# The first microseconds of an encoder layer in a pinned order, with GpSimd on three weight splits and a shorter Newton step

## The chip, the cores and the metric

One core of a Trainium2 chip runs the whole program. Its engines are TensorE (PE; its weight loads are shown as PEld), VectorE (DVE), ScalarE (ACT), GpSimd (POOL) and SyncE (SP), which here only issues DMAs. The metric is the device time of one execution in microseconds (us), the median of the runs.

## The reference, cut to what matters

One layer of an encoder trunk on x of 512 rows by 1024 columns, in float32:

```python
h = rms_norm(x, norm_mix_pre)              # x * rsqrt(mean(x*x) + 1e-6) * g
z = h @ w_in                               # 1024 x 10240
za, zb, q, k, v, su, sv, gl = split(z)
a = za * sigmoid(zb)                       # then a depthwise convolution, layer norm, silu
y_a = a @ w_proj_conv
y_b = rms_norm(diff_attention(q, k, v)) @ w_proj_attn
y_c = spatial_gating(gelu(su), layer_norm(gelu(sv))) @ w_proj_sgu
mix = (g_a * y_a + g_b * y_b + g_c * y_c) @ w_out      # g: sigmoid gates from gl
x = x + rms_norm(mix, norm_mix_post)
f = square(relu(rms_norm(x, norm_ffn_pre) @ w_ffn_up)) @ w_ffn_down
x = x + rms_norm(f, norm_ffn_post)
```

## The kernel before

**Matrix products.** Every operand of a large product is split into a high part, rounded by ScalarE to the matmul's input type, and a low part, the difference, made by VectorE. A product is then three matmuls: high by high, high by low, low by high (`mm3`). A "unit" (`unit_gen`) is a 128-column block of weights against all 512 rows of h, eight steps of three matmuls. A weight block of 128 x 1024 numbers goes through `load_to` (L139 to L152): a DMA on SP's queue into `raw` (L149), the high part `w_hi` on ScalarE (L150), the low part `w_lo` on VectorE (L151). There are three buffers each for raw, high and low. `take` hands out the next blocks and loads ahead. The list `specs` holds the order of all weight blocks; its first three are the pair zb, za of convolution channel block 0 and zb of block 1.

**Order.** A scheduler puts each engine's instructions in order by their place in the program, their readiness and priorities. TensorE's matmuls and transposes are pinned in program order. The helper `keep_in_program_order` ties an instruction behind the one that was written before it on the same engine.

**The head.** ScalarE's queue loads the norm's scales `gpre`, one row copied to all 128 partitions (L271). VectorE clears a tile `zero`, and TensorE multiplies it 26 times as a warm-up (`keep_warm`, L277). SP issues the four 128-row tiles of x (`xx`, L287), with the first weight block behind tile 1 (`W0AT = 1`), the other weight blocks after tile 3.

`norm_x(t)` then norms a tile of x: square with the row sum on ScalarE (L297), `rstd_of`, and the scaling by the row's factor and `gpre` on VectorE (`hs`, L303). `to_T` turns the tile with eight transposes on TensorE (L62), in two halves of a PSUM bank each. ScalarE writes each half's high part `hh` (L223), VectorE its low part `hl` (L224). Tiles 0 and 1 come first, each followed by a few warm-up matmuls of `zero`. Then come the first units on columns 0 to 255, which are tiles 0 and 1: unit 0, norm of tile 2, unit 1, norm of tile 3, unit 2. The second halves of the three units follow, on columns 256 to 511. Unit 0's first half has its own order: eight matmuls of high by high, then eight with the weight's low part, then eight with `hl`. For tiles 2 and 3 a hand-written edge puts the square behind the last `hh` of the tile two before.

**The root.** `rstd_of` (L196) gives 1/sqrt(scale * ss + eps): v on VectorE (L199), ScalarE's root (L201), VectorE's reciprocal (L203) as the first guess, then a Newton step in three VectorE instructions (L206, L210, L211): s = v * r * r, s = 1.5 - 0.5 * s, r = r * s. Where n > 1 the first of them takes two. `eps_with` (L190) adds the first half of a mean to eps, for rows whose squares come in two halves: the norm behind w_out (L815 to L818, its tiles then scaled in L827, turned by `to_T`) and the last norm (`finish`, L1247 to L1258), where VectorE scales and adds (`us`, L1257) and the output is stored.

**Other work on GpSimd.** The constants, the identity for the transposes, seven small loads into `prow` and `cw` (L331 to L339), the padding of `apad` (L359, L360), four small loads for lambda (L187) and an iota (L434).

Of the kernel before, what the change touches and what calls it, by code (L numbers as in the profile page):

```python
# [26 lines left out]
EPS = 1e-6  # L27
# [14 lines left out]
W0AT = 1  # L42
# [6 lines left out]
def encoder_layer(ctx: ExitStack, tc: tile.TileContext, a: dict, out: bass.AP):  # L49
    nc = tc.nc  # L50
    vec, act, pool = nc.vector, nc.scalar, nc.gpsimd
# [15 lines left out]
    def f32(ap):  # L67
        return ap.bitcast(F32)
# [70 lines left out]
    def load_to(n):  # L139
        while len(loaded) < min(n, len(specs)):  # L140
# [10 lines left out]
            vec.tensor_tensor(lo, raw, f32(hi[:, :]), op=ALU.subtract)  # L151
# [38 lines left out]
    def eps_with(p, ss, scale):  # L190

        e = p.tile([P, 1], F32, tag="rs_e", bufs=4, name="rs_e")
        vec.tensor_scalar(e, ss, scale, EPS, op0=ALU.mult, op1=ALU.add)
        return e

    def rstd_of(p, ss, scale, eps=EPS, eps_tile=None, n=1, steps=1):  # L196

        v = p.tile([P, n], F32, tag=f"rs_v{n}", bufs=4 if n == 1 else 1, name="rs_v")
        vec.tensor_scalar(v, ss, scale, eps, op0=ALU.mult, op1=ALU.add)  # L199
        s = p.tile([P, n], F32, tag=f"rs_s{n}", bufs=4 if n == 1 else 1, name="rs_s")  # L200
        act.activation(s, ss, AF.Sqrt, bias=eps_t if eps_tile is None else eps_tile, scale=scale)  # L201
        r = p.tile([P, n], F32, tag=f"rs_r{n}", bufs=4 if n == 1 else 1, name="rs_r")
        vec.reciprocal(r, s)  # L203
        for _ in range(steps):
            if n == 1:
                vec.scalar_tensor_tensor(s, v, r, r, op0=ALU.mult, op1=ALU.mult)  # L206
            else:
                vec.tensor_tensor(s, v, r, op=ALU.mult)
                vec.tensor_tensor(s, s, r, op=ALU.mult)
            vec.tensor_scalar(s, s, -0.5, 1.5, op0=ALU.mult, op1=ALU.add)  # L210
            vec.tensor_tensor(r, r, s, op=ALU.mult)  # L211
        return r

    def to_T(src, hi, lo, tt):
        for half in range(2):
            b = bank("b")
            for j in range(4):
                kt = half * 4 + j
                pe.transpose(b[:, j * P:(j + 1) * P], src[:, kt * P:(kt + 1) * P], ident)
            b3 = b.rearrange("p (k t) -> p k t", t=P)  # L220
            c = slice(half * 4, half * 4 + 4)
            tk = slice(tt * P, (tt + 1) * P)
            ev = act.activation(hi[:, c, tk], b3, AF.Copy)  # L223
            vec.tensor_tensor(lo[:, c, tk], b3, f32(hi[:, c, tk]), op=ALU.subtract)  # L224
        return ev.ins

    def mm3(o, s, m, first, last):

# [39 lines left out]
    hl = KOf(held("hl", "hl", F32R))  # L268
    with mk("p0") as p0:
        gpre = p0.tile([P, D], F32, tag="gpre", name="gpre")  # L270
        act.dma_start(gpre, a["norm_mix_pre"].partition_broadcast(P))  # L271
        warm = p0.tile([P, 1], F32, tag="warm", name="warm")
        act.activation(warm, eps_t, AF.Sqrt)
        zero = p0.tile([P, S], F32R, tag="zero", name="zero")
        vec.memset(f32(zero[:, :]), 0.0)

        def keep_warm(n):  # L277

            b = bank("b")
            for _ in range(n):  # L280
                pe.matmul(b, zero[:, 0:P], zero, start=True, stop=True)

        keep_warm(26)
        xt = []
        for t in range(TT):
            xx = p0.tile([P, D], F32, tag="xx", bufs=4, name="xx")
            nc.sync.dma_start(xx, x[t * P:(t + 1) * P, :])  # L287
            xt.append(xx)
            if t == W0AT:
                load_to(1)  # L290

        evac = {}

        def norm_x(t):
            sq = p0.tile([P, D], F32, tag="sq", bufs=2, name="sq")
            ss = p0.tile([P, 1], F32, tag="ss", bufs=4, name="ss")
            i = act.activation(sq, xt[t], AF.Square, accum_out=ss)  # L297
            if t > 1:
                tc.add_manual_dep(i.ins, evac[t - 2].name, mybir.DependencyInfo(
                    mybir.DependencyClass.NoSync, mybir.DependencyReason.DATA), reason="order")  # L300
            r = rstd_of(p0, ss, 1.0 / D)
            hs = p0.tile([P, D], F32, tag="hs", bufs=2, name="hs")
            vec.scalar_tensor_tensor(hs, xt[t], r, gpre, op0=ALU.mult, op1=ALU.mult)  # L303
            evac[t] = to_T(hs, hh, hl, t)


        hT = (hh, hl)
        norm_x(0)
        keep_warm(3)
        norm_x(1)  # L310
        keep_warm(2)
        first = take(3, 0)
        fb = [bank("a") for _ in first]
        for n, w in enumerate(first):
            if n == 0:

                for i, (sw, m) in enumerate(((0, 0), (1, 0), (0, 1))):
                    for kt in range(KT):
                        pe.matmul(fb[0][:, 0:256], w[sw][:, kt], hT[m][:, kt, 0:256], start=i + kt == 0,
                                  stop=(i, kt) == (2, KT - 1))  # L320
            else:
                run(unit_gen(fb[n][:, 0:256], w, hT, slice(0, 256)))
            if n < 2:
                norm_x(2 + n)
        for n, w in enumerate(first):
            run(unit_gen(fb[n][:, 256:512], w, hT, slice(256, 512)))


        rowsrc = [("conv_b", 8), ("conv_ln_g", 8), ("conv_ln_b", 8), ("b_gate", 24), ("subln_g", 1), ("sgu_b", 8)]
        prow = p0.tile([P, P], F32, tag="prow", name="prow")  # L330
        pool.memset(prow, 0.0)  # L331
        off, col = 0, {}
        for n, k in rowsrc:
            pool.dma_start(prow[off:off + k, :], a[n].rearrange("(r c) -> r c", c=P) if len(a[n].shape) == 1 else a[n])
            col[n] = off
            off += k
        cw = p0.tile([32, D], F32, tag="cw", name="cw")
        pool.memset(cw, 0.0)
        pool.dma_start(cw[0:CK, :], a["conv_w"])  # L339
        pcol = cq.tile([P, P], F32, tag="pcol", name="pcol")  # L340
        b = bank("b")
        pe.transpose(b[:, 0:P], prow, ident)
        for c in range(KT):
            pe.transpose(b[:, P + c * 32:P + (c + 1) * 32], cw[:, c * P:(c + 1) * P], ident[0:32, 0:32])
        vec.tensor_copy(pcol, b[:, 0:P])
        convw = cq.tile([P, KT, 32], F32, tag="convw", name="convw")
        vec.tensor_copy(convw, b[:, P:P + KT * 32].rearrange("p (k j) -> p k j", j=32))

        def pc(n, i=0):
            return pcol[:, col[n] + i:col[n] + i + 1]  # L350
# [203 lines left out]
    for h in range(H):  # L554
        n = 0
# [230 lines left out]
    with mk("p4") as p4:  # L786
# [21 lines left out]
        for t in range(TT):  # L808
            for i in range(4):
                out_mm(b1, t, i, ws[i])  # L810
                if (t, i) in TURN:
                    to_T(h2s[TURN[t, i]], h2h, h2l, TURN[t, i])
            ss = p4.tile([P, 2], F32, tag="ss", bufs=4, name="ss")
            u, jk = wk[:, t], p4.tile([P, D], F32, tag="jk", bufs=3, name="jk")
            act.activation(jk[:, 0:512], b0[t], AF.Square, accum_out=ss[:, 0:1])  # L815
            e = eps_with(p4, ss[:, 0:1], 1.0 / D)
            act.activation(jk[:, 512:], b1[t], AF.Square, accum_out=ss[:, 1:2])
            r = rstd_of(p4, ss[:, 1:2], 1.0 / D, e, e)  # L818
            for i, bs in enumerate((b0, b1)):
# [7 lines left out]
            vec.scalar_tensor_tensor(jk, u, r2, gpre2, op0=ALU.mult, op1=ALU.mult)  # L827
            h2s.append(jk)
# [412 lines left out]
    def finish(nh, t, xs=None):  # L1241
# [9 lines left out]
        if nh == 0:  # L1251
            es.append(eps_with(cp, ss[:, t, 0:1], 1.0 / D))
            return
        r = rstd_of(cp, ss[:, t, 1:2], 1.0 / D, es[t], es[t])
        for e, i in ((nc.sync, 0), (act, 1)):
            hf = slice(i * 512, (i + 1) * 512)
            vec.scalar_tensor_tensor(us[t // 2][:, t % 2, hf], us[t // 2][:, t % 2, hf], r, xs[t // 2][:, t % 2, hf], op0=ALU.mult, op1=ALU.add)  # L1257
# [80 lines left out]
```

## Time and profile before

| | us |
|---|---|
| median of 3 runs | 1060.11 |
| lowest, highest | 1059.85, 1064.0 |
| profiled execution | 1059.99 |
| its span | 1058.2 |
| TensorE busy | 1042.6 |
| VectorE, ScalarE, GpSimd busy | 827.0, 580.5, 24.3 |

The span runs from the first to the last instruction of the profiled execution. The execution's own time is 1.8 us longer than it. Matmuls are pipelined and their ends are modelled, so the busy time of TensorE says that it was occupied, not that it ran at its peak.

A row of the timeline has the start, the duration, the engine, the line, the operation, the tile written and the tiles read, the shape and the count. At its end stands in brackets the engine's idle time before it, with what ended it. A row of the DMA view has the tile, the queue, the count, the size and the time from issue to landing.

### The profile page before, as it was taken

To read this page: it belongs to the slowest core of one execution; us is meant where nothing else is said; L and a number is where in the kernel's file an instruction comes from. 1 tells how busy PE (TensorE), PEld (TensorE's weight loads), DVE (VectorE), ACT (ScalarE), POOL (GpSimd) and SP (SyncE) were. 2 spreads that over 40 slices of the span, in tenths; PEclk is the share of its full clock that TensorE was granted. 3 is DMA by queue.
4 is the path that set the end of the run, shared out by engine and by line. 5 is a ranking of instruction groups with operands and counts; after the bars stand their busy time and mean duration, and the time that the engine had idled before them with its cause. 6 is when DMAs were issued, how large, how long until landed. Compare 5 with 4: busy or idle time off the path is not lost.

```text
span 1058.2 us, 14724 instructions
## 1 busy us (share of the span) xinstructions
PE 1042.6 (99%) x5688; PEld 900.0 (85%) x5688; DVE 827.0 (78%) x1296; ACT 580.5 (55%) x902; POOL 24.3 (2%) x41
## 2 busy tenths in 40 slices
PE   8999999999999999999999999999999999999997
PEld 7989898888878888888888888888999999888885
DVE  6696887968997697999899546457988889867746
ACT  5456677766673752344322493344677787555531
POOL 3000000000000000000000000000000001100000
PEclk9999999999999999999999999999999999999999
DMA  7342323223232333322333214463343319724532
GB/s 227 84 139 61 100 81 100 80 81 87 73 120 87 92 112 90 99 81 80 100 100 99 80 45 135 132 226 138 112 150 101 122 43 265 150 80 139 178 121 80
DMA packets 138391, 118.15 MB, mean 112 GB/s; under 512 B 4166, under 2 KB 116850, under 8 KB 138321
## 3 DMA queue, kind: packets, MB, share of 16 engines
q1 hardware_dynamic: 133120, 103.82, 32.1%
q0 software_dynamic: 4480, 11.82, 4.8%
q10 hardware_dynamic: 720, 1.57, 0.4%
q8 instruction: 44, 0.72, 0.3%
q14 instruction: 27, 0.21, 0.1%
HBM read 108.81 MB, written 4.19 MB: 107 GB/s over the span
## 4 chain that ended last, share of the span: by engine, by line
PE 91%; DVE 5%; ACT 2%; issue 1%; DMA 1%; DVEq 0%; ACTq 0%
PE ps_a L58 69%; PE ps_b L58 19%; PE ps_b L62 3%; DVE w_lo L951 1%; DMA xx<-in_x_dram 1%; DVE us L1257 0%; DVE w_lo L151 0%; ACT y L751 0%; DVE hs L303 0%; DVE jk L827 0%; PE ps_a L62 0%; DVE hl L224 0%; ACT jk L825 0%; DVE jk L1247 0%; DVE rs_s L206 0%
## 5 line engine op out<-in xcount | busy, mean ns | idle before, releaser
L150 ACT ACTIVATE w_hi<-w_raw 128x1024 fp32r<-128x1024 f32 x116 | 122.9, 1059 | 214.0 <-PE ps_a L58 177.4
L58 PE MATMUL ps_a<-hh,w_hi 128*128 128x512 f32 (+1 forms) x536 | 205.4, 385 | 0.0
L58 PE MATMUL ps_a<-hh,w_lo 128*128 128x512 f32 (+1 forms) x536 | 202.9, 381 | 0.0
L58 PE MATMUL ps_a<-hl,w_hi 128*128 128x512 f32 (+1 forms) x536 | 202.5, 380 | 0.0
L372 DVE SCALAR_TENSOR_TENSOR acc<-apad,convw,acc 128x512 f32<-128x512 f32 x232 | 173.5, 748 | 5.0
L151 DVE TENSOR_TENSOR w_lo<-w_raw,w_hi 128x1024 fp32r<-128x1024 f32 x116 | 141.5, 1220 | 41.5 <-ACT w_hi L150 41.2
L58 PEld LDWEIGHTS ps_a<-hh,w_lo 128*128 128x128 f32 x536 | 100.3, 188 | 19.6
L58 PEld LDWEIGHTS ps_a<-hl,w_hi 128*128 128x128 f32 x536 | 100.4, 188 | 18.3
L58 PEld LDWEIGHTS ps_a<-hh,w_hi 128*128 128x128 f32 x536 | 100.4, 188 | 18.2
L58 PE MATMUL ps_a<-ring,w_hi 128*128 128x256 f32 x336 | 57.9, 276 | 0.0
L58 PEld LDWEIGHTS ps_a<-ring,w_hi 128*128 128x128 f32 x336 | 50.6, 188 | 0.0
L58 PE MATMUL ps_a<-h2h,w_lo 128*128 128x256 f32 x176 | 48.8, 277 | 1.4 <-DVE w_lo L951 1.4
L58 PE MATMUL ps_a<-w_hi,hh 128*128 128x256 f32 (+1 forms) x160 | 49.7, 311 | 0.0
L58 PE MATMUL ps_a<-h2h,w_hi 128*128 128x256 f32 x176 | 49.0, 278 | 0.0
L58 PE MATMUL ps_a<-h2l,w_hi 128*128 128x256 f32 x176 | 48.8, 277 | 0.0
L58 PE MATMUL ps_a<-w_hi,hl 128*128 128x256 f32 (+1 forms) x160 | 48.7, 304 | 0.0
L58 PE MATMUL ps_a<-w_lo,hh 128*128 128x256 f32 (+1 forms) x160 | 48.6, 304 | 0.0
L507 ACT ACTIVATE e<-ps_b,m 128x512 f32<-128x512 f32 x64 | 43.4, 681 | 7.3 <-DVE m L503 7.0
L58 PE MATMUL ps_a<-ring,w_lo 128*128 128x256 f32 x168 | 46.5, 277 | 0.2 <-DVE w_lo L951 0.2
L58 PE MATMUL ps_a<-w_hi,ring 128*128 128x512 f32 x144 | 45.5, 389 | 0.0
L503 DVE CUSTOM_DVE_ANT_0 ps_b<-ps_b,al 128x512 f32<-128x512 f32 x64 | 43.5, 698 | 0.5 <-PE ps_b L58 0.2
L951 DVE TENSOR_TENSOR w_lo<-w_raw,w_hi 128x1024 fp32r<-128x1024 f32 x28 | 33.7, 1220 | 8.3 <-ACT w_hi L947 8.3
(304 smaller groups left out, 2431.6 us busy)
## 6 DMA issues: line engine op xcount, KB each, us to landing
w_raw<-in_w_in_dram SPq DMA_DIRECT2D x80, 512.0 KB, 3.7
w_raw<-in_w_ffn_up_dram SPq DMA_DIRECT2D x32, 512.0 KB, 4.6
w_raw<-in_w_ffn_down_dram SPq DMA_DIRECT2D x28, 512.0 KB, 4.1
w_raw<-in_w_proj_attn_dram SPq DMA_DIRECT2D x8, 512.0 KB, 4.0
w_raw<-in_w_proj_sgu_dram SPq DMA_DIRECT2D x8, 512.0 KB, 4.1
w_raw<-in_w_proj_conv_dram SPq DMA_DIRECT2D x8, 512.0 KB, 4.1
w_raw<-in_w_out_dram SPq DMA_DIRECT2D x8, 512.0 KB, 3.6
t<-in_w_ffn_down_dram SPq DMA_DIRECT2D x8, 512.0 KB, 5.7
```

The source lines that it names most:

```text
L58: return tc.keep_in_program_order(nc.tensor.matmul(*args, **kw))
L62: return tc.keep_in_program_order(nc.tensor.transpose(*args, **kw))
L150: act.activation(hi, raw, AF.Copy)
L151: vec.tensor_tensor(lo, raw, f32(hi[:, :]), op=ALU.subtract)
L372: vec.scalar_tensor_tensor(o, apad[:, c, j:j + S], convw[:, c, j:j + 1], acc, op0=ALU.mult, op1=ALU.add)
L503: vec.tensor_tensor_reduce(b, b, nal[:, 384 - q * P:896 - q * P], 1.0, 3.0e38, ALU.add, ALU.min, m)
L507: act.activation(e, b, AF.Exp, bias=m, scale=-1.0, accum_out=l)
L951: order(vec.tensor_tensor(lo, raw, f32(hi[:, :]), op=ALU.subtract))
```

## The change

- **Loads.** `gpre` is issued by SP behind tiles 0 and 1 of x, no longer by ScalarE. Raw weight block 0 follows it, then tile 2, block 1, tile 3, block 2.
- **Order.** The square, the root, the scaling, the first three weight splits, `hh` and `hl` are pinned in the order written. ScalarE has: square 0, root 0, square 1, root 1, hi 0, hh 0, hh 1, square 2, root 2, hi 1, square 3, root 3, hi 2, hh 2, hh 3. VectorE has: root and hs of tile 0, root and hs of tile 1, hl 0, hl 1, root and hs of tile 2, root and hs of tile 3, hl 2, hl 3. TensorE's order stays.
- **Low parts.** The low parts of the first three weight blocks are made by GpSimd (`pool.tensor_tensor`).
- **Newton.** v is made with the factor -0.5, so a step is s = v * r * r and r = (s + 1.5) * r, one instruction fewer. `eps_with` gives eps and -0.5 * eps, one VectorE instruction more.

```diff
+    def first_raw():
+        raw = wp.tile([P, 1024], F32, tag="raw", bufs=3, name="w_raw")
+        nc.sync.dma_start(raw.rearrange("p (k c) -> p k c", c=P), specs[len(heads)])
+        heads.append(raw)
+    def first_parts(n, eng):
+        hi = wp.tile([P, 1024], F32R, tag="hi", bufs=3, name="w_hi")
+        lo = wp.tile([P, 1024], F32R, tag="lo", bufs=3, name="w_lo")
+        eng(act.activation(hi, heads[n], AF.Copy))
+        pool.tensor_tensor(lo, heads[n], f32(hi[:, :]), op=ALU.subtract)
+        loaded.append([t.rearrange("p (k c) -> p k c", c=P) for t in (hi, lo)])
+        return loaded[-1]
...
-        return e
+        eh = p.tile([P, 1], F32, tag="rs_h", bufs=4, name="rs_h")
+        vec.tensor_scalar(eh, e, -0.5, None, op0=ALU.mult)
+        return e, eh
...
-        vec.tensor_scalar(v, ss, scale, eps, op0=ALU.mult, op1=ALU.add)
+        eng(vec.tensor_scalar(v, ss, -0.5 * scale, both[1], op0=ALU.mult, op1=ALU.add))
...
-            vec.tensor_scalar(s, s, -0.5, 1.5, op0=ALU.mult, op1=ALU.add)
-            vec.tensor_tensor(r, r, s, op=ALU.mult)
+            eng(vec.scalar_tensor_tensor(r, s, 1.5, r, op0=ALU.add, op1=ALU.mult))
...
-        act.dma_start(gpre, a["norm_mix_pre"].partition_broadcast(P))
...
             if t == W0AT:
-                load_to(1)
+                nc.sync.dma_start(gpre, a["norm_mix_pre"].partition_broadcast(P))
+                first_raw()
+            elif t > W0AT:
+                first_raw()
...
-        norm_x(0)
+        first = []
+        h0 = scaled(0, root(0))
+        r = root(1)
+        first.append(first_parts(0, pinned))
+        h1 = scaled(1, r)
+        to_T(h0, hh, hl, 0, pinned)
         keep_warm(3)
-        norm_x(1)
+        to_T(h1, hh, hl, 1, pinned)
         keep_warm(2)
-        first = take(3, 0)
+        h2_ = scaled(2, root(2))
+        first.append(first_parts(1, pinned))
+        h3_ = scaled(3, root(3))
+        first.append(first_parts(2, pinned))
...
             if n < 2:
-                norm_x(2 + n)
+                to_T((h2_, h3_)[n], hh, hl, 2 + n, pinned)
+        taken[0] = 3
```

Here `root(t)` is the square with `rstd_of`, `scaled(t, r)` the scaling, both pinned, and `to_T` pins its `hh` and `hl`.

More of the change, by code (lines that the diff above doesn't have):

```diff
@@ L152, in load_to @@
             loaded.append((hi.rearrange("p (k c) -> p k c", c=m), lo.rearrange("p (k c) -> p k c", c=m)))
+    heads = []
+    def first_raw():
[9 more added lines that the diff above has]
+        return loaded[-1]
     def take(m=1, ahead=2):
@@ L193, in eps_with, with rstd_of @@
         vec.tensor_scalar(e, ss, scale, EPS, op0=ALU.mult, op1=ALU.add)
-        return e
-    def rstd_of(p, ss, scale, eps=EPS, eps_tile=None, n=1, steps=1):
+        eh = p.tile([P, 1], F32, tag="rs_h", bufs=4, name="rs_h")
+        vec.tensor_scalar(eh, e, -0.5, None, op0=ALU.mult)
+        return e, eh
+    def rstd_of(p, ss, scale, eps=EPS, eps_tile=None, n=1, steps=1, eng=lambda i: i):
+        both = eps_tile if eps is None else (eps_tile, -0.5 * eps)
         v = p.tile([P, n], F32, tag=f"rs_v{n}", bufs=4 if n == 1 else 1, name="rs_v")
-        vec.tensor_scalar(v, ss, scale, eps, op0=ALU.mult, op1=ALU.add)
+        eng(vec.tensor_scalar(v, ss, -0.5 * scale, both[1], op0=ALU.mult, op1=ALU.add))
         s = p.tile([P, n], F32, tag=f"rs_s{n}", bufs=4 if n == 1 else 1, name="rs_s")
-        act.activation(s, ss, AF.Sqrt, bias=eps_t if eps_tile is None else eps_tile, scale=scale)
+        eng(act.activation(s, ss, AF.Sqrt, bias=eps_t if both[0] is None else both[0], scale=scale))
         r = p.tile([P, n], F32, tag=f"rs_r{n}", bufs=4 if n == 1 else 1, name="rs_r")
-        vec.reciprocal(r, s)
+        eng(vec.reciprocal(r, s))
         for _ in range(steps):
             if n == 1:
-                vec.scalar_tensor_tensor(s, v, r, r, op0=ALU.mult, op1=ALU.mult)
+                eng(vec.scalar_tensor_tensor(s, v, r, r, op0=ALU.mult, op1=ALU.mult))
             else:
@@ L209, in rstd_of, with to_T @@
                 vec.tensor_tensor(s, s, r, op=ALU.mult)
-            vec.tensor_scalar(s, s, -0.5, 1.5, op0=ALU.mult, op1=ALU.add)
-            vec.tensor_tensor(r, r, s, op=ALU.mult)
+            eng(vec.scalar_tensor_tensor(r, s, 1.5, r, op0=ALU.add, op1=ALU.mult))
         return r
-    def to_T(src, hi, lo, tt):
+    def to_T(src, hi, lo, tt, eng=lambda i: i):
         for half in range(2):
@@ L222, in to_T @@
             tk = slice(tt * P, (tt + 1) * P)
-            ev = act.activation(hi[:, c, tk], b3, AF.Copy)
-            vec.tensor_tensor(lo[:, c, tk], b3, f32(hi[:, c, tk]), op=ALU.subtract)
-        return ev.ins
+            eng(act.activation(hi[:, c, tk], b3, AF.Copy))
+            eng(vec.tensor_tensor(lo[:, c, tk], b3, f32(hi[:, c, tk]), op=ALU.subtract))
     def mm3(o, s, m, first, last):
@@ L289, in encoder_layer, with root, scaled @@
             if t == W0AT:
-                load_to(1)
-        evac = {}
-        def norm_x(t):
+                nc.sync.dma_start(gpre, a["norm_mix_pre"].partition_broadcast(P))
+                first_raw()
+            elif t > W0AT:
+                first_raw()
+        pinned = tc.keep_in_program_order
+        def root(t):
             sq = p0.tile([P, D], F32, tag="sq", bufs=2, name="sq")
             ss = p0.tile([P, 1], F32, tag="ss", bufs=4, name="ss")
[L297 to L301, printed above, removed]
+            pinned(act.activation(sq, xt[t], AF.Square, accum_out=ss))
+            return rstd_of(p0, ss, 1.0 / D, eng=pinned)
+        def scaled(t, r):
             hs = p0.tile([P, D], F32, tag="hs", bufs=2, name="hs")
-            vec.scalar_tensor_tensor(hs, xt[t], r, gpre, op0=ALU.mult, op1=ALU.mult)
-            evac[t] = to_T(hs, hh, hl, t)
+            pinned(vec.scalar_tensor_tensor(hs, xt[t], r, gpre, op0=ALU.mult, op1=ALU.mult))
+            return hs
         hT = (hh, hl)
-        norm_x(0)
+        first = []
[4 more added lines that the diff above has]
+        to_T(h0, hh, hl, 0, pinned)
         keep_warm(3)
-        norm_x(1)
+        to_T(h1, hh, hl, 1, pinned)
         keep_warm(2)
-        first = take(3, 0)
+        h2_ = scaled(2, root(2))
+        first.append(first_parts(1, pinned))
+        h3_ = scaled(3, root(3))
+        first.append(first_parts(2, pinned))
         fb = [bank("a") for _ in first]
@@ L817, in encoder_layer @@
             act.activation(jk[:, 512:], b1[t], AF.Square, accum_out=ss[:, 1:2])
-            r = rstd_of(p4, ss[:, 1:2], 1.0 / D, e, e)
+            r = rstd_of(p4, ss[:, 1:2], 1.0 / D, None, e)
             for i, bs in enumerate((b0, b1)):
@@ L1253, in finish @@
             return
-        r = rstd_of(cp, ss[:, t, 1:2], 1.0 / D, es[t], es[t])
+        r = rstd_of(cp, ss[:, t, 1:2], 1.0 / D, None, es[t])
         for e, i in ((nc.sync, 0), (act, 1)):
```

## The prediction

> **What bounds the kernel now.** I read the page first, then busy time by stretch, then the timeline of the first 36 us engine by engine, then the ends of the chain that ended last.
>
> ```profile
> span 1058.2 us, 14724 instructions
> PE 1042.6 (99%) x5688; PEld 900.0 (85%) x5688; DVE 827.0 (78%) x1296; ACT 580.5 (55%) x902; POOL 24.3 (2%) x41
> ...
> PE 91%; DVE 5%; ACT 2%; issue 1%; DMA 1%; DVEq 0%; ACTq 0%
> ```
> TensorE is busy 1042.6 of 1058.2 us and carries 91% of the chain. So a microsecond counts only where TensorE waits, or where its busy time is not work of the task. The stretches show where that is (after the stretch and its length stand the busy times of TensorE, its weight loads, VectorE, ScalarE and GpSimd, then the granted clock, the DMA share and GB/s):
>
> ```profile
> 9.80:14.10 4.30, 3.35 (x21) 2.65 (x22) 4.16 (x9) 4.13 (x8) 0.00 (x0) 1.00 1.08 350
> ...
> 17.00:24.20 7.20, 5.14 (x43) 4.80 (x42) 5.69 (x11) 1.66 (x5) 0.72 (x3) 1.00 0.46 148
> ...
> 35.80:1050.00 1014.20, 1010.61 (x5478) 871.67 (x5478) 803.15 (x1248) 563.03 (x872) 15.34 (x17) 1.00 0.37 109
> ```
> From 35.80 to 1050 us TensorE stands for 3.59 us in all; from 17.00 to 24.20 alone for 2.06. The TensorE timeline shows the head in detail (L62 are transposes; matmuls of "zero" are the warm-up, which computes nothing; in brackets the wait and who ended it):
>
> ```profile
> 1.46 8.04 PE L58 MATMUL ps_b<-zero 128*128 128x512 f32 x26 [1.46 <-DVE zero L275]
> ...
> 11.93 1.06 PE L62 MATMUL ps_b<-ident,hs 128*128 128x128 f32 x8 [0.33 <-DVE hs L303]
> 13.58 0.73 PE L58 MATMUL ps_b<-zero 128*128 128x512 f32 x2 [0.58 <-DVE hl L224]
> 14.14 1.11 PE L58 MATMUL ps_a<-hh,w_hi 128*128 128x256 f32 x8
> 15.09 1.12 PE L58 MATMUL ps_a<-hh,w_lo 128*128 128x256 f32 x8
> 16.05 1.12 PE L58 MATMUL ps_a<-hl,w_hi 128*128 128x256 f32 x8
> 18.69 1.06 PE L62 MATMUL ps_b<-ident,hs 128*128 128x128 f32 x8 [1.52 <-DVE hs L303]
> 23.16 1.09 PE L62 MATMUL ps_b<-ident,hs 128*128 128x128 f32 x8 [0.54 <-DVE hs L303]
> ...
> 35.60 0.27 PE L62 MATMUL ps_b<-ident,prow 128*128 128x128 f32 x1
> ```
> Work of the task on weights starts at 14.14 and the three first units end at 35.60. Between lie 21.46 us, 2.06 of them the two waits for hs (1.52 and 0.54), so 19.40 us are work. Two things can move that end: an earlier 14.14, and smaller waits. After it the shift is carried to the end of the kernel, because the rest has only those 3.59 us of waits and is paced by TensorE.
>
> **The change: the head.** What feeds 14.14 is seen on ScalarE and VectorE:
>
> ```profile
> 6.07 1.06 ACT L297 ACTIVATE sq<-xx 128x1024 f32<-128x1024 f32 x1 [3.39 <-DMA xx<-in_x_dram]
> ...
> 7.54 1.06 ACT L297 ACTIVATE sq<-xx 128x1024 f32<-128x1024 f32 x1
> ...
> 9.40 1.06 ACT L150 ACTIVATE w_hi<-w_raw 128x1024 fp32r<-128x1024 f32 x1 [0.38 <-DMA w_raw<-in_w_in_dram]
> 10.51 1.09 ACT L223 ACTIVATE hh<-ps_b 128x512 fp32r<-128x512 f32 x2
> 11.48 1.06 ACT L297 ACTIVATE sq<-xx 128x1024 f32<-128x1024 f32 x1
> 12.43 0.20 ACT L297 ACTIVATION_READ_ACCUMULATOR sq<-xx 128x1 f32 x1
> 12.60 1.08 ACT L223 ACTIVATE hh<-ps_b 128x512 fp32r<-128x512 f32 x2
> ...
> 14.77 0.28 ACT L201 ACTIVATE rs_s<-ss,eps_t 128x1 f32<-128x1 f32 x1
> ```
> ```profile
> 8.41 1.28 DVE L303 SCALAR_TENSOR_TENSOR hs<-xx,rs_r,gpre 128x1024 f32<-128x1024 f32 x1
> 9.61 0.15 DVE L199 TENSOR_SCALAR rs_v<-ss 128x1 f32<-128x1 f32 x1
> ...
> 10.50 1.28 DVE L303 SCALAR_TENSOR_TENSOR hs<-xx,rs_r,gpre 128x1024 f32<-128x1024 f32 x1
> 11.70 1.22 DVE L151 TENSOR_TENSOR w_lo<-w_raw,w_hi 128x1024 fp32r<-128x1024 f32 x1
> 12.84 2.48 DVE L224 TENSOR_TENSOR hl<-ps_b,hh 128x512 fp32r<-128x512 f32 x4
> ```
> Here L297 is the square, L201 the root (0.28 us), L150 and L151 make a weight's high and low part (hi, lo), L223 and L224 a tile's (hh, hl). The square of tile 2 (11.48, with its read-out 1.15 us) stands ahead of tile 1's hh at 12.60, and the weight's low part (11.70) ahead of the hl that frees the bank of the last warm-up at 13.58. The new order takes both out: hh of tile 1 goes straight behind hh of tile 0, and the low part goes to GpSimd.
>
> The loads come first in time. x and gpre issued together:
>
> ```profile
> gpre<-in_norm_mix_pre_dram ACTq DMA_DIRECT2D x1, 512.0 KB, 5.5
> xx<-in_x_dram SPq DMA_DIRECT2D x1, 512.0 KB, 5.3
> ```
> Tile 0 of x ends ScalarE's wait at 6.07, gpre lands 0.2 later, tile 1 of x is there by 7.54 and raw 0 at 9.40; 512 KB at the 350 GB/s of the full stretch (share 1.08) are 1.5 us, one place in the line. The scales move from ScalarE's queue to SP's, past two tiles of x: one issue more stands on SP ahead of raw 0, x 2 and the rest, but the same four transfers are ahead of or equal to raw 0, so I keep 9.40 for it. By places, x 0 lands near 4.5, x 1 near 6.0, gpre near 7.5. So hs 0 is then bound by gpre, not by its root: 7.5 to 8.8 instead of 8.41 to 9.69 (1.28). The small steps of tile 1's root follow it (five of them cost 0.8 us between 9.61 and 10.50; four remain, 0.6), and hs 1 runs 9.4 to 10.7.
>
> Now in order. hi 0 at 9.40 as before, hh 0 from 10.5, both halves to 11.5 (1.09). Transposes of tile 1 at 10.8 (0.15 behind hs, as 11.93 against 11.78), so hh 1 follows at 11.5 to 12.6. hl 0's first half waits for hh, 11.1 to 11.7, and frees the warm-up's bank: the warm-up starts at 11.8 and unit 0 0.56 later (13.58 to 14.14 now), at **12.36: 1.78 earlier**. The first 26 warm-up matmuls end at 9.50, after hs 0 is ready, and cost nothing as long as hh 0 waits for hi 0 anyway.
>
> GpSimd's price is not in the trace: no subtraction of two tensors runs there. Nearest rows:
>
> ```profile
> 0.74 0.20 POOL masks.py:197 MEMSET ident<- 128x128 f32 x1 [0.29 <-POOLq L1319]
> ...
> 1.19 0.29 POOL masks.py:199 TENSOR_SCALAR_AFFINE_SELECT ident<-ident 128x128 f32<-128x128 f32 x1
> ...
> 4.76 0.97 POOL L338 MEMSET cw<- 32x1024 f32 x1
> ```
> A pass that reads nothing takes 0.97 for 1024 columns: the lower end. One input costs 0.29-0.20 = 0.09 more for 128 columns, 0.7 for 1024 columns; two inputs give 0.97+1.4, so 2.3 to 2.4, and I take 2.3. The upper end is the select's whole 0.29 per 128 columns (2.3 for 1024) and one more input, 3.0. The low part is not below zero cost to others: it gives VectorE 1.22 us three times.
>
> lo 0 runs 10.5 to 12.8 and is first used 0.95 behind unit 0's start (14.14 to 15.09), at 13.3: covered with 0.5 to spare; at 3.0 it costs 0.2. Unit 0 ends at 12.36+3.03 = 15.39. ScalarE goes on from hh 1: square of tile 2 12.6 to 13.7, its root to 14.0, hi 1 to 15.0, square 3 to 16.0, root to 16.3, hi 2 to 17.3. VectorE: root steps 14.0 to 14.7, hs 2 to 16.0, so tile 2's transposes start at 16.15: a wait of 0.76 where 1.52 was. lo 1 is ready at 15.0+2.3 = 17.3; unit 1 starts at about 17.0 and reads it with its third matmul: no wait at 2.3, 0.7 at 3.0. hs 3 ends at 18.3 and lo 2 at 19.6, both before tile 3's transposes come up near 20: the wait of 0.54 goes. So the units end at 12.36+19.40+0.76 = 32.52 instead of 35.60: **3.08 us**, 2.2 with GpSimd at 3.0. What is late next is hs 2, behind ScalarE's square and root.
>
> Queued behind the three passes on GpSimd are the padding of apad, four small loads and an iota:
>
> ```profile
> 23.30 0.20 POOL L359 MEMSET apad<- 128x120 f32 x1 [16.76 <-DVE hs L303]
> ```
> Before, they stand behind hs 3, and they still come after it; their first reader is the gated output of unit 1, behind the units' end. That leaves over 10 us of cover in both kernels. SP's fourth weight load waits for raw 0, free at 12.8 by lo 0 instead of 12.92: even.
>
> A rule speaks against the GpSimd part, beside these rows, in which no reading GpSimd pass meets a two-input VectorE pass. The Trainium skill, "SBUF — State Buffer", section "Who interferes with whom", says that GpSimd shares a port pair with VectorE, and that a VectorE instruction with two SBUF inputs and a GpSimd instruction that reads SBUF shut each other out for whole instructions. By it the head's 3.1 would be about 1.2; no run here shows it yet.
>
> **The change: Newton steps.** A step has two instructions instead of three, with the -0.5 put into v, off the chain beside ScalarE's root. The halved epsilon is one more tiny VectorE instruction per tile where a mean is taken in two halves, also earlier than its use. It counts where a chain ends TensorE's waits or the kernel:
>
> ```profile
> 1053.01 0.22 DVE L206 SCALAR_TENSOR_TENSOR rs_s<-rs_v,rs_r 128x1 f32<-128x1 f32 x1
> 1053.27 0.15 DVE L210 TENSOR_SCALAR rs_s<-rs_s 128x1 f32<-128x1 f32 x1
> 1053.45 0.16 DVE L211 TENSOR_TENSOR rs_r<-rs_r,rs_s 128x1 f32<-128x1 f32 x1
> 1053.65 1.42 DVE L1257 SCALAR_TENSOR_TENSOR us<-us,rs_r,xs 128x512 f32<-128x512 f32 x2
> ```
> ```profile
> 612.98 1.20 PE L62 MATMUL ps_b<-ident,y 128*128 128x128 f32 x9 [0.29 <-ACT y L751]
> 737.23 1.06 PE L62 MATMUL ps_b<-ident,jk 128*128 128x128 f32 x8 [0.61 <-DVE jk L827]
> ```
> In the tail 0.18 goes (1053.27 to 1053.45) and the last step grows from 0.16 to 0.22: 0.13 (0.12 to 0.18). At 737 the root is followed by jk, for which TensorE waits 0.61: between 0 (other VectorE work fills the same slots) and 0.61; I take 0.20, near the one instruction saved. At 612: 0 to 0.13, I take 0.05. Sum **0.38**, bounds 0.12 to 0.9.
>
> **The sum.** The profiled execution took 1059.99 us (span 1058.2 and 1.8 around it); 1059.99-3.08-0.38 = 1056.5. The median of the runs is 1060.11, 0.1 higher, so I forecast 1056.6.
>
> **Rivals.** *The ports are shared.* hs 2 (14.7 to 16.0) holds lo 1 back to 16.0, so it ends at 18.3 and unit 1 at about 21.0. Tile 3's root steps, due at 16.5, wait until 18.3. If lo 2 then gets in between them, hs 3 ends at 22.4, its transposes start at 22.5 and the units end near 34.95; if VectorE goes first, near 33.8. Gain of the head 0.65 to 1.8, middle 1.2: 1058.4. For it: the page; against: nothing in this trace, which cannot show it. *The ports are shared and a pass takes over 2.8 us* (slower). In the first of those orders two passes lie on the path, so the end of the units moves twice as fast as the pass: from 34.95 at 2.3 to 36.0 at 2.8, where Newton's 0.38 is used up, and 36.4 at my upper end of 3.0. There it gives 1060.4, at 3.5 us 1061.4. Against it: it needs a pass beyond the middle of the rows. *The head is bound by something that stays:* raw 0 lands at 9.40 and everything hangs on hi 0. If SP's extra issue, or reading one row 128 times, delays the line, all of it slips by that delay; at 3.1 us, two more places in the line, only Newton is left: 1059.6.
>
> **How the numbers follow.** Forecast 0.46 (1055.2 to 1057.6: the lower end with Newton at 0.9 and half a place in the line won, the upper with GpSimd at 3.0), shared ports 0.33 (1057.8 to 1059.4), shared and long 0.08 (above 1060.2), loads late 0.06 (1059.6), the other instructions' order shifted elsewhere by more than 1 us 0.07. The range 1055.2 to 1060.2 leaves out the slow rival and about half of the last. 0.5% is 5.3 us, about what a measurement of this kernel can tell from no change: 1054.8 and 1065.4 are the borders, and none of the cases reaches either with its terms alone. So within 0.5% has 0.92, faster 0.05, slower 0.03, both from the last case and from landings that I have placed badly.
>
> **What would show it.** Right: gpre lands near 7.5 and hs 0 starts on it; hh 1 directly follows hh 0 on ScalarE; unit 0 starts near 12.4; GpSimd passes of 2.3 us; one wait of about 0.8 ahead of tile 2's transposes and none ahead of tile 3's; prow's transpose near 32.5; two instructions between reciprocal and us in the tail. The sharing rival shows as lo 1 or a 128x1 step that starts late or lasts over 1 us while the other engine runs. Wrong altogether: prow's transpose at 35 or later, or an early gain that is gone by 1050 us.

## The result, and the profile after

The changed kernel takes 1077.72 us (median of 4 runs, 1075.82 to 1079.5) against 1060.17 (1059.85 to 1064.0) before: ratio 1.0153, interval 1.013 to 1.0177. It is slower by 16 to 18 us, where 1056.6 was forecast and 1060.2 was the upper end of the range.

Executions of most kernels here fall on two levels about 4 us apart, for a reason that stays open (before near 1060.1 and 1064.2); "lower" below is the median of the runs of the lower one, and as before's profile (1059.99 us) is of the lower level and after's (1079.5 us) of the upper one, some 4 of the 19.5 us between their spans are not the change's.

The head of after's page:

```profile
span 1077.7 us, 14704 instructions
PE 1063.9 (99%) x5688; PEld 905.9 (84%) x5688; DVE 826.7 (77%) x1275; ACT 580.4 (54%) x902; POOL 31.6 (3%) x44
PE 93%; DVE 4%; ACT 2%; issue 1%; DVEq 0%; ACTq 0%
```

The span is 19.5 us longer and TensorE is busy 21.3 us longer, for the same 5688 matmuls. VectorE and ScalarE are as busy as before. So TensorE doesn't wait longer: it works longer. The page's groups say on what:

```profile
L58 PE MATMUL ps_a<-hh,w_hi 128*128 128x512 f32 (+1 forms) x536 | 207.8, 390 | 0.0
L58 PE MATMUL ps_a<-hh,w_lo 128*128 128x512 f32 (+1 forms) x536 | 205.3, 385 | 0.9 <-POOL w_lo L166 0.9
L58 PE MATMUL ps_a<-hl,w_hi 128*128 128x512 f32 (+1 forms) x536 | 205.2, 385 | 0.0
```

Before, the same three groups:

```profile
L58 PE MATMUL ps_a<-hh,w_hi 128*128 128x512 f32 (+1 forms) x536 | 205.4, 385 | 0.0
L58 PE MATMUL ps_a<-hh,w_lo 128*128 128x512 f32 (+1 forms) x536 | 202.9, 381 | 0.0
L58 PE MATMUL ps_a<-hl,w_hi 128*128 128x512 f32 (+1 forms) x536 | 202.5, 380 | 0.0
```

Each matmul lasts 4 to 5 ns longer, in all three groups. A stretch in the middle of the kernel, 450 to 550 us, shows the pace more clearly than the share of busy time does. First before, then after (after the stretch and its length: busy time and count of TensorE, its weight loads, VectorE, ScalarE, GpSimd; granted clock, DMA share, GB/s):

```profile
450.00:550.00 100.00, 100.00 (x458) 82.75 (x457) 91.06 (x120) 36.28 (x47) 0.00 (x0) 1.00 0.31 90
```
```profile
450.00:550.00 100.00, 100.00 (x448) 81.13 (x447) 89.52 (x117) 35.63 (x46) 0.00 (x0) 1.00 0.30 89
```

TensorE is 100% busy in both, at a granted clock of 1.00 in both, and does 448 matmuls where it did 458: 2.2% fewer. The same shows in the chain of waits of each kernel as one piece of 36 matmuls of 512 columns. Before, then after:

```profile
985.69 8.16 PE ps_b L58 x36
```
```profile
1003.45 8.40 PE ps_b L58 x36
```

That is 226.7 ns and 233.3 ns a matmul. The loss is no single event: the same TensorE instruction comes 0.8 us earlier than before at 33 us, 0.5 later at 175, 4.6 at 425, 8.9 at 600, 11.5 at 728, 19.7 at the end. It grows where most matmuls have 512 columns. The 3.9 us that come between 745 and 880 us, where they have 256 columns, are the 4 us that are not the change's: the profile of the kernel before with a shift of 256 bytes (below) has 3.7 there too.

What was forecast of the head did mostly happen. VectorE of after:

```profile
7.97 1.28 DVE L323 SCALAR_TENSOR_TENSOR hs<-xx,rs_r,gpre 128x1024 f32<-128x1024 f32 x1 [1.37 <-DMA gpre<-in_norm_mix_pre_dram]
...
14.64 0.22 DVE L227 SCALAR_TENSOR_TENSOR rs_s<-rs_v,rs_r 128x1 f32<-128x1 f32 x1
14.90 0.16 DVE L231 SCALAR_TENSOR_TENSOR rs_r<-rs_s,rs_r 128x1 f32<-128x1 f32 x1
15.09 1.28 DVE L323 SCALAR_TENSOR_TENSOR hs<-xx,rs_r,gpre 128x1024 f32<-128x1024 f32 x1
16.43 0.15 DVE L219 TENSOR_SCALAR rs_v<-ss 128x1 f32<-128x1 f32 x1
16.76 0.16 DVE L223 RECIPROCAL rs_r<-rs_s 128x1 f32<-128x1 f32 x1 [0.18 <-ACT rs_s L221]
16.96 1.66 DVE L227 SCALAR_TENSOR_TENSOR rs_s<-rs_v,rs_r 128x1 f32<-128x1 f32 x1
18.65 2.32 DVE L231 SCALAR_TENSOR_TENSOR rs_r<-rs_s,rs_r 128x1 f32<-128x1 f32 x1
21.00 1.28 DVE L323 SCALAR_TENSOR_TENSOR hs<-xx,rs_r,gpre 128x1024 f32<-128x1024 f32 x1
```

GpSimd of after:

```profile
10.87 2.55 POOL L166 TENSOR_TENSOR w_lo<-w_raw,w_hi 128x1024 fp32r<-128x1024 f32 x1 [7.12 <-ACT w_hi L165]
...
15.69 0.51 POOL L369 DMA_DIRECT2D cw<-in_conv_w_dram  x1 [0.29 <-POOL cw L368]
16.21 4.74 POOL L166 TENSOR_TENSOR w_lo<-w_raw,w_hi 128x1024 fp32r<-128x1024 f32 x2
```

TensorE of after:

```profile
12.67 1.18 PE L58 MATMUL ps_a<-hh,w_hi 128*128 128x256 f32 x8
...
16.43 1.09 PE L62 MATMUL ps_b<-ident,hs 128*128 128x128 f32 x8 [0.69 <-DVE hs L323]
...
18.65 0.39 PE L58 MATMUL ps_a<-hh,w_lo 128*128 128x256 f32 x1 [0.89 <-POOL w_lo L166]
...
22.35 1.09 PE L62 MATMUL ps_b<-ident,hs 128*128 128x128 f32 x8 [0.82 <-DVE hs L323]
...
34.79 0.27 PE L62 MATMUL ps_b<-ident,prow 128*128 128x128 f32 x1
```

Two steps on one column of 128 numbers take 0.22 and 0.16 us for tile 2 and 1.66 and 2.32 us for tile 3. The first ends with GpSimd's second pass (18.6), the second with its third (20.95). Both read two tiles. The two instructions ahead of them, which read one tile each, ran beside the same second pass (it began at 16.21) in their usual 0.15 and 0.16. So the order that the sharing rival described came about, and the three units end 0.81 us earlier than before instead of 3.08.

### The profile page after: what moved, and what is told of

It is laid out like the page before. It is cut to its first block, busy times and chain, and to the rows that moved or that the text cites. A ratio compares the mean times of both kernels' runs of the same rounds, so it can differ in the third digit from the quotient of the medians.

```text
span 1077.7 us, 14704 instructions
## 1 busy us (share of the span) xinstructions
PE 1063.9 (99%) x5688; PEld 905.9 (84%) x5688; DVE 826.7 (77%) x1275; ACT 580.4 (54%) x902; POOL 31.6 (3%) x44
## 4 chain that ended last, share of the span: by engine, by line
PE 93%; DVE 4%; ACT 2%; issue 1%; DVEq 0%; ACTq 0%
PE ps_a L58 70%; PE ps_b L58 19%; PE ps_b L62 3%; DVE w_lo L981 1%; ACT y L781 0%; DVE wk L852 0%; PE ps_a L62 0%; DVE rs_r L231 0%; DVE rs_s L227 0%; ACT L221 0%; DVE jk L857 0%; DVE w_sum L969 0%; DVE w_lo L151 0%; ACT jk L855 0%; ACT sq L318 0%
## 5 line engine op out<-in xcount | busy, mean ns | idle before, releaser
L150 ACT ACTIVATE w_hi<-w_raw 128x1024 fp32r<-128x1024 f32 x113 | 119.6, 1059 | 226.0 <-PE ps_a L58 194.1
L58 PE MATMUL ps_a<-hh,w_hi 128*128 128x512 f32 (+1 forms) x536 | 207.8, 390 | 0.0
L58 PE MATMUL ps_a<-hh,w_lo 128*128 128x512 f32 (+1 forms) x536 | 205.3, 385 | 0.9 <-POOL w_lo L166 0.9
L58 PE MATMUL ps_a<-hl,w_hi 128*128 128x512 f32 (+1 forms) x536 | 205.2, 385 | 0.0
L151 DVE TENSOR_TENSOR w_lo<-w_raw,w_hi 128x1024 fp32r<-128x1024 f32 x113 | 137.9, 1221 | 43.2 <-ACT w_hi L150 42.4
L981 DVE TENSOR_TENSOR w_lo<-w_raw,w_hi 128x1024 fp32r<-128x1024 f32 x28 | 33.7, 1220 | 8.5 <-ACT w_hi L977 8.5
```

Of the source, the lines that this page charges most:

```text
L58: return tc.keep_in_program_order(nc.tensor.matmul(*args, **kw))
L150: act.activation(hi, raw, AF.Copy)
L981: order(vec.tensor_tensor(lo, raw, f32(hi[:, :]), op=ALU.subtract))
```

## The experiments

Two questions: why TensorE's pace is lower in the whole kernel, and what the head and the Newton step are worth without that.

The theory for the pace is the **place of buffers in SBUF**. `eps_with` has a new tile, `rs_h`: one number per partition, four buffers of 32 bytes, 128 bytes in all. In the last norm it lies in the pool `cp`, which stands behind the weight buffers' pool `wp` and ahead of h's and nearly all the rest. In the built programs the first buffer of h lies at byte 55296 of a partition before and 55424 after; the first `w_hi` lies at 29184 in both. Their distance was a multiple of 256 bytes and is now 128 more. The second half of h begins 64 bytes into its own buffer, so its numbers, too, lay at a multiple of 256 bytes from the weights. The rival theory is the new order itself: other instructions beside the matmuls, or the shorter step. The kernel has a pad of 448 bytes (`pad1`) between `cp` and h's pool, and one of 384 (`pad0`) ahead of `wp`; both are one number to change.

**The change with the buffers back in their places.**

```diff
-    pad(ctx, "pad1", 448)
+    pad(ctx, "pad1", 320)
```

> The whole change, with the filler tile pad1 cut from 448 to 320 bytes, so that every buffer behind it stands at the SBUF address that it has in the kernel before. Theory P (places): the new tile rs_h in the pool of constants moves all buffers behind it by 128 bytes against the weight buffers, and matmuls that read one operand from each side then come 232 instead of 227 ns apart. It expects 227 ns again and about 1059 us: 1060.1 less the 0.8 that the head of the changed kernel won by 35 us, less 0.1 in the tail. Rival O (order): the new head or the GpSimd passes put the rest into a slower rhythm; it expects 1076 to 1080 us as the change has.

Measured: 1059.8 us (10 runs; lower 1059.67), before 1060.37 (lower 1060.30), ratio 0.9987 (0.9969 to 1.0005). The pace is back, by the window and the chain of waits:

```profile
450.00:550.00 100.00, 100.00 (x458) 82.74 (x457) 91.05 (x120) 36.70 (x47) 0.00 (x0) 1.00 0.31 90
```
```profile
1000.57 8.16 PE ps_b L58 x36
```

All of the loss is gone with 128 bytes of a pad, every instruction of the change still there. Between the profiled executions of the two, 1063.83 and 1079.5 us, lie 15.7 us.

**The kernel before, shifted by 128 bytes.** The kernel before with `pad1` at 576 and nothing of the change.

```diff
-    pad(ctx, "pad1", 448)
+    pad(ctx, "pad1", 576)
```

> The kernel before, with nothing but the filler tile pad1 grown from 448 to 576 bytes: all buffers behind it move by 128 bytes, the weight buffers stay. Theory P expects the whole loss with no other edit: 232 to 233 ns between 512-column matmuls and 1076 to 1081 us. Rival O expects 1060 us.

Measured: 1080.06 us (4 runs), ratio 1.016 (1.0138 to 1.0182). The window and the chain:

```profile
450.00:550.00 100.00, 100.00 (x449) 81.07 (x448) 89.23 (x117) 35.63 (x46) 0.00 (x0) 1.00 0.29 85
```
```profile
1004.12 8.37 PE ps_b L58 x36
```

449 matmuls in 100 us, without one instruction of the change. With the run above this shows the cause from both sides, and the rival of the new order falls. Another rival would be the other engines or the DMAs, whose reads and writes may collide with TensorE's at the new places. The traces of before and after speak against it. Take the 512-column matmuls between 100 and 600 us, each from its start to the next one's. Those with neither VectorE nor ScalarE busy meanwhile came 226.7 ns apart before (92 of them) and 232.7 after (82). Those with no DMA packet moving meanwhile came 227.7 and 232.4 ns apart (over 900 in each).

**Everything shifted by 128 bytes, weights too.** Is it the address or the distance?

```diff
-    pad(ctx, "pad0", 384)
+    pad(ctx, "pad0", 512)
```

> The kernel before, with the filler tile pad0, which lies ahead of the weight buffers, grown from 384 to 512 bytes: weights and everything behind them move together by 128 bytes. If it is the place of the two operands relative to each other (theory P) nothing changes: 1060 us and 227 ns. If it is the absolute address of a buffer, such as a start at a multiple of 512 bytes (rival A), it is as slow as the shift of the rest alone: 1076 to 1081 us.

Measured: 1062.6 us (10 runs), ratio 1.0008 (0.9991 to 1.0024). The matmuls of the chain stand 226.7 ns apart again:

```profile
1001.88 8.16 PE ps_b L58 x36
```

The distance to the weights decides, not the address of h. The profiled execution is 1.3 us later at the end of the head (the prow transpose at 36.89 instead of 35.60) and still 1.3 later at 745 us. The second weight block came late in it: its high part waited 0.87 us for its load and started at 14.68 instead of 13.80. Why the load was late was not followed.

**Half the shift, and twice.** The kernel before with `pad1` at 512 (64 bytes) and at 704 (256 bytes).

> The kernel before with pad1 grown by 64 bytes: everything behind it moves by 64 bytes against the weight buffers. Theory P expects the spacing of the 512-column matmuls to depend on this distance alone. If any distance off a multiple of 128 or 256 bytes is slow, it is slow here too (232 ns, 1076 to 1081 us); the kernel before has one half of h at distance 0 and the other at -64 modulo 512 and is fast on both, which speaks for a window, and 64 bytes may lie in it: then 1060 us.

> The kernel before with pad1 grown by 256 bytes. If the pattern repeats every 256 bytes, this is as fast as before: 227 ns and 1060 us. If it repeats at 512 bytes or more, it is slow, between 1070 and 1085 us, and which side of the two reads is late shows in the spacing.

Measured: with 64 bytes 1075.47 us (2 runs), ratio 1.0128 (1.0097 to 1.016); with 256 bytes 1060.2 us (8 runs), ratio 0.9996 (0.998 to 1.0012). The window and the chain with 64 bytes. In the window, where most matmuls read h, 453 are done in 100 us, half of the loss at 128 bytes; the last product has lost as much as there:

```profile
450.00:550.00 100.00, 100.00 (x453) 82.14 (x453) 90.02 (x118) 35.06 (x45) 0.00 (x0) 1.00 0.29 86
```
```profile
999.30 8.40 PE ps_b L58 x36
```

And with 256 bytes, the chain:

```profile
1000.85 8.16 PE ps_b L58 x36
```

The window and the last product of the 64-byte kernel differ in which operand the weights are. In most products the weights are the stationary operand (the 128x128 block that is loaded) and h the moving one (512 columns); between 300 and 600 us these matmuls came 229 to 230 ns apart (before 227). In the last product, and in one product with h between 311 and 358 us, the weights move, and the spacing is 233 to 234 ns (before 226 to 229). So the shift by 64 bytes costs about half where it raised the address of the moving operand, and all where it raised that of the stationary one. The expectation's "-64" is the start of the buffer that holds h's second half; the numbers in it start 64 bytes later, so before's 227 ns say nothing of a distance of -64.

**The weights shifted instead of h.** `pad0` at 512 and `pad1` at 320: the weight buffers move by 128 bytes, and with them the small tiles and the identity in `cp`; h's buffers and everything behind them stay.

> The kernel before with pad0 grown by 128 bytes and pad1 cut by 128: the weight buffers alone move, all else stays where it was. Theory P, by now with a pattern of 256 bytes (a shift of 64 or 128 was slow, 256 was not), expects the loss from this side too: about 232 ns and 1075 to 1081 us. If only the place of h, the ring and the other large buffers counts and not the distance, it stays at 1060.

Measured: 1081.47 us (2 runs), ratio 1.0194 (1.0161 to 1.0226). The window and the chain:

```profile
450.00:550.00 100.00, 100.00 (x449) 81.16 (x448) 89.30 (x116) 36.39 (x48) 0.00 (x0) 1.00 0.29 85
```
```profile
1006.14 8.40 PE ps_b L58 x36
```

Moving either side of the pair does it. Of this profile's loss 1.9 us stand at the end of the head already (the prow transpose at 37.45), again with a late load of the second weight block.

**The Newton step alone**, on the kernel before, with `pad1` at 320 so that the places stay.

```diff
+        eh = p.tile([P, 1], F32, tag="rs_h", bufs=4, name="rs_h")
+        vec.tensor_scalar(eh, e, -0.5, None, op0=ALU.mult)
...
-            vec.tensor_scalar(s, s, -0.5, 1.5, op0=ALU.mult, op1=ALU.add)
-            vec.tensor_tensor(r, r, s, op=ALU.mult)
+            vec.scalar_tensor_tensor(r, s, 1.5, r, op0=ALU.add, op1=ALU.mult)
```

> Only the shorter Newton steps in the kernel before, with pad1 at 320 bytes so that all places stay. Theory P expects 1059.6 to 1060.1 us: 0.13 us less in the tail, at most 0.6 less ahead of the second norm's last transposes. If the shorter steps or the extra halved epsilon were what disturbs the rest (rival N) it is near 1077.

Measured: 1062.0 us (10 runs; lower 1059.96), before 1060.37 (lower 1060.30), ratio 1.0001 (0.9983 to 1.0019). A gain of 0.34 can't be told from none here. TensorE's waits of this kernel show what was won and lost:

```profile
PE ps_b L62 <- ACT y L753: 0.8, 1, 0.8
...
PE ps_a L58 <- DVE h2l L226: 0.2, 1, 0.2
```

Before, y cost 0.3 and jk 0.6. The wait for jk is gone, with 0.2 for its low part in its place, and the wait for y has grown by 0.5.

**Two of three low parts back on VectorE.** The whole change with places kept, block 0's low part on GpSimd, those of blocks 1 and 2 on VectorE, pinned behind hs 2 and hs 3.

```diff
-        pool.tensor_tensor(lo, heads[n], f32(hi[:, :]), op=ALU.subtract)
+        if n == 0:
+            pool.tensor_tensor(lo, heads[n], f32(hi[:, :]), op=ALU.subtract)
+        else:
+            eng(vec.tensor_tensor(lo, heads[n], f32(hi[:, :]), op=ALU.subtract))
```

> The whole change at the old places (pad1 at 320 bytes), with the low parts of weight blocks 1 and 2 back on VectorE, behind hs 2 and hs 3; block 0 stays on GpSimd. Theory S (shared port): the two 128x1 steps of tile 3's root that lasted 1.66 and 2.32 us stood still for GpSimd's passes; it expects 0.22 and 0.16 there, hs 3 to end near 19.4 instead of 22.3, tile 3's transposes without a wait, the units' end near 32.7 instead of 34.8, and about 2 us less than the change at the old places: 1057.6 us. Rival L (late inputs): these steps waited for their own inputs, from ScalarE; then they stay long and the time stays near 1059.7.

Measured: **1057.46 us** (8 runs, 1057.15 to 1058.03), before 1060.28, ratio 0.9958 (0.9942 to 0.9974): better than both kernels. VectorE, tile 3's steps and what follows:

```profile
17.69 0.22 DVE L230 SCALAR_TENSOR_TENSOR rs_s<-rs_v,rs_r 128x1 f32<-128x1 f32 x1
17.94 0.16 DVE L234 SCALAR_TENSOR_TENSOR rs_r<-rs_s,rs_r 128x1 f32<-128x1 f32 x1
18.14 1.29 DVE L326 SCALAR_TENSOR_TENSOR hs<-xx,rs_r,gpre 128x1024 f32<-128x1024 f32 x1
19.34 1.22 DVE L169 TENSOR_TENSOR w_lo<-w_raw,w_hi 128x1024 fp32r<-128x1024 f32 x1
```

TensorE of the same kernel:

```profile
12.68 1.17 PE L58 MATMUL ps_a<-hh,w_hi 128*128 128x256 f32 x8
...
20.31 1.03 PE L62 MATMUL ps_b<-ident,hs 128*128 128x128 f32 x8
...
32.69 0.27 PE L62 MATMUL ps_b<-ident,prow 128*128 128x128 f32 x1
```

The steps last 0.22 and 0.16 again, hs 3 comes 2.9 us earlier than in after, and no wait stands ahead of tile 3's transposes. Of the 2.91 us by which the units end earlier than before, 2.8 arrive in the time.

**All three on VectorE**, the first between the hl of tiles 0 and 1.

> As the last one, with block 0's low part on VectorE too, between tile 0's hl and tile 1's hl: GpSimd makes none. Theory S expects the same short steps; what VectorE now does in between puts hs 2 about 0.7 us later, so the units end near 33.4 and the time is near 1058.3 us. Rival L: near 1059.7 or more.

Measured: 1058.13 us (12 runs), ratio 0.9972 (0.9959 to 0.9985); the prow transpose at 33.75. By the medians the first low part is better on GpSimd by 0.7 (1057.46 against 1058.13). There it takes 2.5 us beside little that reads two tiles from SBUF, and VectorE is spared 1.22 us between tile 0's hl and tile 1's. The prow transposes lie 1.06 apart, but 0.55 of that stands at unit 0's start already (13.23 against 12.68): raw 0's high part started 0.56 later in this execution, with the loads in the same order.

**The scales loaded first**, as before the change, on the kernel with two low parts on VectorE.

```diff
+        act.dma_start(gpre, a["norm_mix_pre"].partition_broadcast(P))
...
-                nc.sync.dma_start(gpre, a["norm_mix_pre"].partition_broadcast(P))
```

> The run with two low parts on VectorE, with the scales' load moved back to ScalarE's queue at the very start. By the loads' places in the line hs 0 then starts near 8.4 instead of 8.0 and hs 1, unit 0 and the units' end follow by up to 0.4 us, unless raw 0 holds hh 0 back anyway: 1057.5 to 1057.9 us. Rival: the later arrival of x 0 and x 1 costs the roots 1 us or more: 1058.5.

Measured: 1057.65 us (12 runs), before 1059.99, ratio 0.9972 (0.9958 to 0.9986). hs 0 starts at 8.20 instead of 7.97 and the prow transpose stands at 32.92 instead of 32.69. The order of the loads is worth 0.2 us of the 2.9 by which the head ends earlier. The first low part on GpSimd has 0.5 to 0.7 by the experiment before this one. What is left, about 2, is put down to the pinned order and the shorter root steps, which no run separates.

**GpSimd's small loads first.** In after, two loads of prow, the clearing of cw and its load stand between the first and the second low part, and the second begins at 16.21 directly behind them. Hs 2 also runs until 16.37. To tell the two apart, these stand ahead of the first low part, in the kernel with the buffers back in their places. The diff shows one of the lines that were moved and pinned:

```diff
-            pool.dma_start(prow[off:off + k, :], a[n].rearrange("(r c) -> r c", c=P) if len(a[n].shape) == 1 else a[n])
+            pinned(pool.dma_start(prow[off:off + k, :], a[n].rearrange("(r c) -> r c", c=P) if len(a[n].shape) == 1 else a[n]))
...
-        pool.tensor_tensor(lo, heads[n], f32(hi[:, :]), op=ALU.subtract)
+        eng(pool.tensor_tensor(lo, heads[n], f32(hi[:, :]), op=ALU.subtract))
```

> The change with the pad shortened (as in the run with the buffers back in their places), and on GpSimd the clearing of prow and cw with their seven small loads pinned ahead of the first low part. In that run two of these loads, the clearing and the load of cw stood between lo 0 and lo 1, and lo 1 began at 16.55, directly behind the last of them, while hi 1 was ready at 15.72 and hs 2 ran from 15.45 to 16.73. Two theories of why lo 1 was late. If the queue alone held it: lo 1 begins at about 15.75 and ends near 18.1, TensorE's wait for it (0.90) falls to 0.25 or less, tile 3's root steps and hs 3 come about 0.8 earlier, and the prow transpose stands near 34.3 instead of 35.15; about 0.8 us less than that run, 1058.9. If the shared port also holds it: lo 1 ends no earlier than 16.73 + 2.2 = 18.9, the wait stays at 0.8 to 0.9, the prow transpose stays near 35.1 and the time near 1059.7. By both theories tile 3's two steps of 128x1 still last over 1 us each.

Measured: 1060.2 us (10 runs), before 1060.3, ratio 0.9995 (0.9983 to 1.0008). GpSimd of this kernel, 14 to 18 us, and then VectorE's hs 2:

```profile
15.93 3.16 POOL L166 TENSOR_TENSOR w_lo<-w_raw,w_hi 128x1024 fp32r<-128x1024 f32 x1 [2.31 <-ACT w_hi L165]
```
```profile
15.58 1.28 DVE L323 SCALAR_TENSOR_TENSOR hs<-xx,rs_r,gpre 128x1024 f32<-128x1024 f32 x1
```

The pass now starts when hi 1 is ready, and lasts 3.16 us instead of 2.39: it ends 2.2 us after hs 2 does (19.09 against 16.86). TensorE's wait for it stays at 0.89 and the prow transpose at 35.28. The queue alone was not what held the second pass; hs 2 holds it too.

## Why the prediction was wrong

**The step that failed** is "After it the shift is carried to the end of the kernel, because the rest has only those 3.59 us of waits and is paced by TensorE". That TensorE paces the rest was read rightly, and just for that reason its pace was the one number that the whole sum hung on. It was taken as fixed, because no matmul was changed. `rs_h` was costed as "one more tiny VectorE instruction per tile"; its 128 bytes were not costed at all. They took about 16 us: 1075.9 (lower) for after against 1059.7 (lower) for the same program with its buffers back, and a 512-column matmul came every 232 to 233 ns instead of 227. Of the two signs of "wrong altogether", "an early gain that is gone by 1050 us" is the one that came: 0.8 us early at 33 us, 19.7 late at the end. The last of the rivals, another order of the other instructions (0.07), allowed for a loss elsewhere, but by another cause: with the buffers back that order is kept and the loss is gone.

**The head without low parts** was sized well. gpre landed at 7.97 (7.5), raw 0's high part started at 9.72 (9.40), hh 1 followed hh 0 with 0.21 between them, unit 0 started at 12.67 (12.36). Each is 0.3 to 0.5 late, from the loads on. The wait ahead of tile 2's transposes was 0.69 (0.76).

**GpSimd's pass** was 2.38 to 2.55 us (2.3 taken, 3.0 the upper end). Its duration was about right; what it collides with was not in the sum. The forecast took no wait for the low parts and none at tile 3, and TensorE waited 0.89 and 0.82 there.

**The sharing rival** (0.33) described this head: tile 3's root held back, the third pass getting in between its two steps, hs 3 ending at 22.28 (22.4), the units at 34.79 (34.95). Of the 22.12 us from unit 0's start to there 2.40 are the three waits and 19.72 the rest, where the sum had 19.40 of work. That is not the slower pace: with the buffers back in their places the rest is 19.74. With two low parts on VectorE and one wait it is 19.33. So the 0.3 go with the waits: by the starts of the matmuls each gap is about 0.16 longer than its bracket says. With the places kept, the change gives 1059.7 (lower), where that rival had 1058.4. Its 1.2 us for the head were the middle of two orders, and the order that came was the worse one, with 0.65; the loads were 0.3 to 0.4 later in that execution (the prow transpose at 35.15, 0.45 earlier than before), and Newton gave less. The rule of the Trainium skill, "SBUF — State Buffer", section "Who interferes with whom", agrees with the trace: 128x1 steps of 1.66 and 2.32 us beside a pass against 0.22 and 0.16, and a pass of 3.16 instead of 2.39 that started during hs 2. I had the rule and the right order, and still gave the forecast 0.46. With two of the low parts off GpSimd the units end at 32.69, where the forecast without sharing had 32.52.

**GpSimd's queue** was given wrongly: I named only what stands behind the three passes. Two loads of prow and the clearing and load of cw had moved in between the passes. The last experiment shows that this cost next to nothing, because hs 2 held the second pass about as long: the wait stayed at 0.89.

**Newton** was put at 0.38. The tail won 0.20 (0.13 forecast; 0.18 less 0.06 is 0.12):

```profile
1072.70 0.22 DVE L227 SCALAR_TENSOR_TENSOR rs_s<-rs_v,rs_r 128x1 f32<-128x1 f32 x1
1072.95 0.16 DVE L231 SCALAR_TENSOR_TENSOR rs_r<-rs_s,rs_r 128x1 f32<-128x1 f32 x1
1073.14 1.41 DVE L1287 SCALAR_TENSOR_TENSOR us<-us,rs_r,xs 128x512 f32<-128x512 f32 x2
```

From the first step to `us` are 0.44 us instead of 0.64. The last step took 0.16, not 0.22. At 737 us 0.6 of wait went and 0.2 came (0.20 forecast, 0.61 the bound). At 612 us 0.05 was forecast and the wait grew by 0.5 instead. By these the sum is near 0.1; the lower runs say 0.34, and the interval takes in both.

**What stays open.** Which of TensorE's two reads, of the stationary or of the moving operand, is slowed was not separated, nor which other distances are free; only shifts by 64, 128 and 256 bytes were tried. Matmuls of 256 columns do not follow the same pattern. Between 42 and 216 us those with h stationary and the weights moving came 114 ns apart at a shift of 64 bytes and 118 to 120 without one or at 128. Between 745 and 880 us the change's profile loses nothing against the one with its buffers back.

## What to carry to other kernels

A tile of a few bytes in a pool near the front moves every buffer behind it: after a change that adds or drops a tile, compare the SBUF addresses of the matmuls' operands before and after, and make up the difference with a pad before judging the change. When one engine is 99% busy, compare its pace (the count in a fixed stretch, or the duration of a fixed count), not its share, which was 99% in both kernels here. And hand GpSimd a pass that reads SBUF only where VectorE has no instruction with two inputs in SBUF on the path meanwhile, however small: here a step on 128 numbers lasted 2.32 us instead of 0.16.

## What the runs showed of the hardware that was not expected

- Back-to-back matmuls of 512 columns came 226.7 ns apart in the last product with the operands' buffers as before or moved by 256 bytes against each other, and 232.5 to 233.3 ns apart at 64 and 128 bytes, with the granted clock at 1.00 throughout. Moving both sides by 128 bytes left them at 226.7. In time: 1060.2 at 256 bytes, 1075.5 at 64, 1080.1 and 1081.5 at 128. At 64 bytes the loss was half where the weights were the stationary operand.
- The Trainium skill, "SBUF — State Buffer", section "Who interferes with whom", gives TensorE two independent read ports, for the moving operand and for the weight load, and says that TensorE waits on nobody. Nothing in that rule lets the distance of two buffers matter; here it costs 2.2% of the matmul pace (448 against 458 in 100 us), and the measurement decides.
- GpSimd and VectorE held each other up for whole instructions even where the VectorE instruction had one element per partition: 1.66 and 2.32 us instead of 0.22 and 0.16. The other way, a GpSimd pass that began during a VectorE hs took 3.16 us instead of 2.39, and 3.05 in the kernel with the scales loaded first.
